# Partition sums on float32r halves, a softmax scale moved to ScalarE, and a later finish of one attention unit

## Chip, cores and metric

The kernel runs on one core of one Trainium2 chip. The metric is the device time of one execution in microseconds. The kernel before was run three times; its median is 651.46 us.

## What is computed

Two layers of an encoder on 512 tokens with 1024 features (cut from the reference):

```python
for l in range(DEPTH):                               # DEPTH = 2
    mod = silu(c) @ w_ada[l] + b_ada[l]              # 1024 -> 3072
    shift, scale, gate = split(mod, 3)
    h = rms_norm(x, norm_g[l]) * (1 + scale) + shift
    qa, ka, va, ga, qb, kb, vb, gb, qc, kc, vc, gc = split(h @ w_in[l])     # 3712 columns
    oa = rms_norm(diff_attention(qa, ka, va)) * silu(ga)  # A: 4 heads, p1 - lam * p2
    ob = dilated_attention(qb, kb, vb) * silu(gb)         # B: 6 heads, three window patterns
    oc = retention_bidir(qc, kc, vc) * silu(gc)           # C: 4 heads, chunked, two directions
    x = x + gate * (concat(oa, ob, oc) @ w_out[l])
```

All inputs are float32.

## The kernel before

**Products.** A dense product in float32 is made of three products on float32r: each operand is split into a high part, which ScalarE copies to float32r, and a low part, which VectorE subtracts (`split`, line 575; `Piece.split`, line 294, for weights). `products` (line 337) adds hi*hi, hi*lo and lo*hi in one accumulator of PSUM.

**Stages and groups.** The projection is cut by columns into chunks of 16 groups: 4 blocks of weight rows times 4 token tiles. A group is 6 products (2 row blocks of 128 times 3). In each layer the chunks are C's values and C's q and k (in layer 0 both in one chunk), A unit 0, B unit 0, A unit 1, B unit 1, B unit 2, gate C, then gate B (12 groups, turned), then the output projection (32 groups). A has 2 units of two heads, B has 3. Each chunk's accumulators come from a PSUM pool of 4 (`acc_p`). The scores have a PSUM pool of 2 (`sc_p`), the four-block transposes (`tr4`, line 569) a pool of 1 (`tr_p`), the values times weights one (`pv_p`).

**The plan.** `at(g, fn)` hangs a step behind group number g; `issue` (line 167) emits groups and their steps in that order, so it is a plan written out by hand with offsets such as `START_A1`, `GATE` or `FIN2`. The scheduler of the framework takes this order as a priority: on each engine it issues what is ready by its own model, and holds a step back until the buffers that it writes are free. So a step that stands later in the plan can be issued earlier, and a buffer that is held long moves what comes behind it. Each engine then works its own queue strictly in the issued order.

**Buffers that matter here.** The pool `ep` has five buffers of 128x512 with the tag "e" (line 144). The scores of A take four for a query tile (`Diff.scores`, line 738, tile e), those of B two (`Dilated.scores`, line 799, tile sb); they are free after the transposes of that tile. Also there: oat, oao and oasq (the finish of A's units, lines 755 to 764), cth (the gate of C, line 988) and several short-lived tiles. `out_pair(k)` (line 1018) gives the two float32r halves of a unit's output, in the single buffers s0 to s9, which C used earlier in the layer.

**A's finish.** `Diff.finish` (line 755) copies the output of the attention to oat; `finish2` (line 760), `FIN2` = 4 groups later, transposes it to oao, squares it on GpSimd and forms the norm; `finish3` (line 776), 12 groups later, applies the norm on VectorE and the gate values ga on GpSimd (line 781); `finish4` (line 783), 4 more later, transposes back and splits into the output pair. Both units have the same offsets.

**B's softmax.** For each query tile and head `Dilated.scores` makes the scores on TensorE (lines 802 and 803), adds the mask and takes the maximum in one VectorE instruction (line 807) and lets ScalarE take the exponential. `soft` (line 811) takes the reciprocal of the sum and scales the tile: head 0 on ScalarE, head 1 on VectorE (line 818), as `N_SOFT` is above any query tile. `turn` (line 699) transposes each head's tile, `values` (line 710) multiplies by v.

**Gate C and gate B.** `gate_done` (line 987) reads gate C's accumulator of a token tile: a tanh on ScalarE (cth), then two VectorE instructions. Gate B's products (lines 342 to 344) come next and need free accumulators.

**Sums over partitions.** `ada_steps` (line 455) forms a row of silu(c) @ w_ada: VectorE adds eight scaled weight rows per partition into `ada_acc` (line 474), and `end` (line 477) sums over the partitions and spreads the sum to all of them by one float32 product with a matrix of ones (line 479). It is used for the gate, twice in each layer (`gate_use`, line 1081, whose tile shares the two buffers "ga" with A's gate values), and for the modulation of layer 1, four times (`mod_use`, line 490). `plan_ada` (line 1087) sets its places. The sum stands in a score buffer of PSUM until it is read.

Of the kernel before, what the change touches and what calls it, by code (L numbers as in the profile page):

```python
# [9 lines left out]
F32 = mybir.dt.float32  # L10
# [7 lines left out]
S = 512  # L18
# [26 lines left out]
GATE, GATE_GAP, GATE_END = 55, 24, 18  # L45
GB_OUT = 9
SETUP, TABLES, RET_T, TAB1 = 12, 12, 19, 9      
N_A1, N_B1, N_SOFT = 5, 5, 9
E_T1, E_T2, E_X, E_QF, E_SCALE_A, E_SCALE_B = 1, 1, 1, 0, 0, 0
FIN2, FIN3, FIN4 = 4, 12, 16  # L50
X_BACK = 2


# [81 lines left out]
def encoder(ctx, tc, x, c, norm_g, w_ada, b_ada, w_in, w_out, params, consts, out):  # L135
# [19 lines left out]
    def act(o, i, f=AF.Copy, **kw):  # L155
        A.activation(o, i, f, **kw)  # L156
# [7 lines left out]
    def at(g, fn, *args):  # L164
        plan.setdefault(g, []).append((fn, args))
# [20 lines left out]
    cst = one.tile([P, N_KEEP], F32, name="cst")  # L186
    ones = one.tile([P, P], F32, name="ones")
    V.memset(ones, 1.0)
    nhalf = one.tile([P, 16], F32, name="nhalf")
    V.memset(nhalf, -0.5)  # L190

# [92 lines left out]
    class Piece:  # L284


        def __init__(self, src, n, where=None, gains=(None, None)):
            self.src, self.n, self.where, self.gains = src, n, where, gains
# [166 lines left out]
    def ada_steps(l, cols, use):  # L455

        (c0, n), cnt = cols[0], len(cols)
        step = cols[1][0] - c0 if cnt > 1 else 0
        z = {}

        def load(r):
            def fn():
                raw = z[r] = rp.tile([P, 2, 512], F32, name="raw")
                rows2(raw, w_ada, l * D * 3 * D + r * 3 * D + c0, KD * 3 * D, 3 * D, step, cnt, n)
                if r == 0:
                    a = z["a"] = two.tile([P, 512], F32, name="ada_acc")
                    G.memset(a, 0.0)
                    dma(a[0:1].rearrange("o (j n) -> o j n", j=cnt), dram(b_ada, l * 3 * D + c0, [[0, 1], [step, cnt], [1, n]]))
            return fn

        def add(r):
            def fn():
                for rr in range(2):
                    stt(z["a"], z[r][:, rr], cs[:, r + rr:r + rr + 1], z["a"], OP.mult, OP.add)
            return fn

        def end():
            ps = sc_p.tile([P, 512], F32, name="ada_ps", tag="sc")
            T.matmul(ps, ones, z["a"], start=True, stop=True)
            use(ps)  # L480
        return [load(r) for r in range(0, KD, 2)], [add(r) for r in range(0, KD, 2)], end

    mods = [None] * 4

# [234 lines left out]
                                 start=k == 0, stop=k == NT - 1)  # L719

    class Diff(Attention):
        def __init__(self, unit, g0, gap, oh, ol):
            self.oh, self.ol = oh, ol
            self.m = {}
            super().__init__(unit, g0, gap)

# [26 lines left out]
                self.e[qt, h] = self.m[2 * h]  # L753

        def finish(self, g):
            self.ob = ep.tile([P, S], F32, name="oat", tag="e")
            act(self.ob, self.pv)
            at(g + FIN2, self.finish2, g + FIN2)

        def finish2(self, g):  # L760
            ps = tr4([self.ob[:, tok_(t)] for t in range(NT)])
            o = self.o = ep.tile([P, 8, DV_A], F32, name="oao", tag="e")
            act(o.rearrange("p g d -> p (g d)"), ps.rearrange("p t m -> p (t m)"))
            sq = ep.tile([P, 8, DV_A], F32, name="oasq", tag="e")
            G.tensor_tensor(sq, o, o, OP.mult)
            ss = self.ss = sm.tile([P, 8], F32, name="oass")
            r0 = self.r0 = sm.tile([P, 8], F32, name="oar0")
            V.reciprocal(r0.rearrange("p (t h) -> p t h", h=2), self.ssum[:, :, 0::2])
            V.tensor_reduce(ss, sq, AX.X, OP.add)
            V.tensor_tensor(ss, ss, r0, OP.mult)  # L770
            V.tensor_tensor(ss, ss, r0, OP.mult)
            rms_end(ss, 8, DV_A)
            at(g + FIN3, self.finish3)
            at(g + FIN4, self.finish4)

        def finish3(self):
            o, ss = self.o, self.ss
# [5 lines left out]
        def finish4(self):  # L783
            on = self.o.rearrange("p (t h) d -> p t (h d)", h=2)
            ps = tr4([on[:, t] for t in range(NT)])
            split(self.oh, self.ol, ps.rearrange("p t m -> p (t m)"))

    class Dilated(Attention):
        def __init__(self, unit, g0, gap, ob, sg, out):
# [21 lines left out]
        def soft(self, qt):  # L811
            for h in range(2):
                V.reciprocal(self.s[h], self.s[h])
                sb = self.e[qt, h]
                if h == 0 or qt >= N_SOFT:
                    act(sb, sb, AF.Copy, scale=self.s[h])
                else:
                    V.tensor_scalar(sb, sb, self.s[h], None, OP.mult)

        def finish(self, g):  # L820
            if self.sg:
# [180 lines left out]
    def layer(l):  # L1002
# [15 lines left out]
        def out_pair(k):  # L1018
            oAB[k] = [one.tile([P, S], F32R, name=f"o{k}{z}", tag=f"s{2 * k + z}") for z in range(2)]
            return oAB[k]  # L1020

        def start_a(u, un, g, gap):
            Diff(un, g, gap, *out_pair(u))

        def start_b(u, un, g, gap):

# [58 lines left out]
            return use  # L1085

        def plan_ada(steps, g, gap, g_end=0):
            loads, adds, end = steps
            for i in range(4):
                at(g + gap * i - 6, loads[i])  # L1090
                at(g + gap * i, adds[i])
            at(max(g + gap * 4, g_end), end)
            return g + gap * 4

# [221 lines left out]
```

## Time and profile before

| | |
|---|---|
| three runs | 649.25, 651.46, 651.51 us (median 651.46) |
| the profiled execution | 650.6 us, span 648.7 us |
| mean granted TensorE clock | 0.992 |

The profile shows one execution. Busy shares of the engines are averages over all stages; a table by stretch gives them for one stage. A timeline lists instructions with start and duration in us, and in brackets the idle time of the engine before them with what ended it. Matmuls overlap in the records: the distance of their starts says what one costs in a dense stretch, its duration is longer. The chain of work that ended last gives these distances.

### The profile page before, as it was taken

The numbers are of one execution on the slowest core, as the hardware profiler recorded it, in microseconds if no ns is written. First come the engines' busy times: TensorE is split into PE (matmuls) and PEld (weight loads), VectorE is DVE, ScalarE is ACT, GpSimd is POOL, SyncE is SP. The second block draws the span as 40 slices with busy tenths as digits, with TensorE's granted clock in tenths as the row PEclk, the third lists the DMA queues.
The fourth block names the chain that finished last, engine by engine and source line by source line (L and its number), as shares of the span: only waits on it lengthen the run. The fifth ranks groups of instructions, "written<-read, shape, count | busy, mean of one in ns | idle before, by whom it ended". The sixth has DMA issues, their size and how long they took to land.

```text
span 648.7 us, 10469 instructions
## 1 busy us (share of the span) xinstructions
PE 622.2 (96%) x3487; PEld 512.2 (79%) x3487; DVE 491.8 (76%) x1206; ACT 344.4 (53%) x756; POOL 163.7 (25%) x183
## 2 busy tenths in 40 slices
PE   6899999999999996999999999999999999899997
PEld 1788888987888873677779998997788787677786
DVE  4787676689988987898969364768997997578443
ACT  4855263566646665564424344455756577566410
POOL 1105452514350510200411041633323340020000
PEclk9799999999999999999999999999999999999999
DMA  8998123535555556476643322235565453604211
GB/s 302 295 293 238 55 70 98 135 98 146 150 152 176 141 176 161 160 248 201 216 156 110 90 73 66 71 104 159 134 176 137 135 145 112 161 34 149 80 65 66
DMA packets 87277, 93.03 MB, mean 143 GB/s; under 512 B 7188, under 2 KB 68276, under 8 KB 87224
## 3 DMA queue, kind: packets, MB, share of 16 engines
q1 hardware_dynamic: 87224, 92.37, 48.0%
q8 instruction: 28, 0.46, 0.3%
q14 instruction: 25, 0.20, 0.1%
HBM read 72.42 MB, written 4.19 MB: 118 GB/s over the span
## 4 chain that ended last, share of the span: by engine, by line
PE 79%; DVE 9%; issue 4%; DMA 3%; POOL 3%; ACT 2%; SPq 1%; POOLq 0%; ACTq 0%
PE acc L346 16%; PE acc L348 16%; PE acc L347 16%; PE tr L572 8%; PE pv L718 5%; PE sc L741 2%; DMA x<-in_x_dram 2%; PE acc L344 1%; PE acc L342 1%; PE acc L343 1%; PE sc L802 1%; PE sc L803 1%; DVE wlo L315 1%; PE co L971 1%; DVE pt L708 1%
## 5 line engine op out<-in xcount | busy, mean ns | idle before, releaser
L346 PE MATMUL acc<-whi,hT 128*128 128x384 f32 (+1 forms) x424 | 154.7, 365 | 0.0
L347 PE MATMUL acc<-wlo,hT 128*128 128x384 f32 (+1 forms) x424 | 151.8, 358 | 0.0
L348 PE MATMUL acc<-whi,hL 128*128 128x384 f32 (+1 forms) x424 | 151.8, 358 | 0.0
L315 DVE TENSOR_TENSOR wlo<-raw,whi 128x384 fp32r<-128x384 f32 (+1 forms) x130 | 80.7, 650 | 26.7 <-ACT whi L156 26.4
L199 POOL TENSOR_TENSOR qkss<-qkss,nhalf 128x4 f32<-128x4 f32 (+1 forms) x40 | 52.6, 1315 | 128.3 <-DVE qkss L587 127.3
L346 PEld LDWEIGHTS acc<-whi,hT 128*128 128x128 f32 x424 | 80.0, 189 | 6.1
L348 PEld LDWEIGHTS acc<-whi,hL 128*128 128x128 f32 x424 | 79.8, 188 | 6.2
L347 PEld LDWEIGHTS acc<-wlo,hT 128*128 128x128 f32 x424 | 80.0, 189 | 5.5
L156 ACT ACTIVATE whi<-raw 128x768 fp32r<-128x768 f32 (+2 forms) x67 | 59.5, 890 | 39.7 <-PE acc L348 33.8
L159 DVE SCALAR_TENSOR_TENSOR ada_acc<-raw,cs,ada_acc 128x512 f32<-128x512 f32 x86 | 64.3, 749 | 3.9 <-DMA raw<-in_w_ada_dram 3.3
L156 ACT ACTIVATE e<-sc,mx 128x512 f32<-128x512 f32 x64 | 43.9, 689 | 35.5 <-DVE mx L743 16.9
L743 DVE TENSOR_REDUCE mx<-sc 128x1 f32<-128x512 f32 x64 | 43.5, 685 | 9.5 <-PE sc L741 8.8
L156 ACT ACTIVATE sb<-sb,mx 128x512 f32<-128x512 f32 x48 | 34.4, 717 | 20.4 <-DVE mx L807 20.2
L718 PE MATMUL pv<-pt,v 128*64 128x256 f32 x320 | 38.9, 385 | 1.0 <-DVE pt L708 0.9
L156 ACT ACTIVATE pt<-tr 128x512 f32<-128x512 f32 x40 | 23.8, 596 | 23.1 <-PE tr L572 22.9
L572 PE MATMUL tr<-cst,sb 128*128 128x128 f32 x192 | 30.7, 283 | 5.3 <-DVE nat L159 2.2
L807 DVE CUSTOM_DVE_ANT_0 sb<-sc,cst 128x512 f32<-128x512 f32 x48 | 32.1, 683 | 4.4 <-PE sc L803 2.6
L572 PEld LDWEIGHTS tr<-cst,sb 128*128 128x128 f32 x192 | 21.9, 142 | 16.0 <-ACT pt L156 7.7
L718 PEld LDWEIGHTS pv<-pt,v 128*64 128x64 f32 x320 | 21.2, 136 | 16.2 <-DVE pt L708 5.5
L708 DVE COPY pt<-tr 128x512 f32<-128x512 f32 x40 | 27.4, 684 | 7.8 <-PE tr L572 7.8
L639 POOL TENSOR_TENSOR qkn<-qkraw,qkss 128x256 f32<-128x256 f32 x40 | 30.0, 751 | 5.9 <-DVE qkraw L635 2.0
L741 PE MATMUL sc<-stk,stq 96*128 96x512 f32 x64 | 27.3, 434 | 1.0 <-ACT e L156 0.9
(294 smaller groups left out, 1367.8 us busy)
## 6 DMA issues: line engine op xcount, KB each, us to landing
raw<-in_w_ada_dram SPq DMA_DIRECT2D x64, 256.0 KB, 3.2
raw<-in_w_in_dram SPq DMA_DIRECT2D x48, 192.0 KB, 2.9
raw<-in_w_in_dram SPq DMA_DIRECT2D x24, 384.0 KB, 3.4
raw<-in_w_in_dram SPq DMA_DIRECT2D x32, 256.0 KB, 3.4
raw<-in_w_ada_dram SPq DMA_DIRECT2D x16, 512.0 KB, 5.1
raw<-in_w_out_dram SPq DMA_DIRECT2D x32, 256.0 KB, 3.0
x<-in_x_dram SPq DMA_DIRECT2D x8, 512.0 KB, 4.2
stB<-nat SPq DMA_DIRECT2D x32, 128.0 KB, 2.4
```

Source lines behind the costliest of these rows:

```text
L156: A.activation(o, i, f, **kw)
L159: V.scalar_tensor_tensor(o, a, s, b, op0, op1)
L199: G.tensor_tensor(o, i, nhalf[:, :n], OP.pow)
L315: V.tensor_tensor(l2[:, z], r2[:, z], h2[:, z].bitcast(F32), OP.subtract)
L346: T.matmul(ps, ah, hi[i], start=s_, stop=False)
L347: T.matmul(ps, ah, lo[i], start=False, stop=False)
L348: T.matmul(ps, al, hi[i], start=False, stop=e_)
L572: T.transpose(ps[:, i, :], b, ident)
L708: V.tensor_copy(pt, ps)
L718: T.matmul(self.pv[h * 64:h * 64 + 64, i * 256:i * 256 + 256], self.u.v[:, k, h * 64:h * 64 + 64], self.pt[h][:, k], start=k == 0, stop=k ...
L741: T.matmul(ps, self.u.stq[0:96, m, tok_(qt)], self.u.stk[0:96, m], start=True, stop=True)
L743: V.tensor_reduce(mx, ps, AX.X, OP.max, negate=True)
```

## The change

The sum over partitions is made of two float32r products: a new step `parts`, one group ahead, splits `ada_acc` into a high and a low half (two tiles of the pool `ep`), and `end` multiplies both with ones in float32r. `soft` scales both of B's heads on ScalarE. In A the tiles oat and oao go from the pool `ep` to the single buffers s1 and s0 (unit 0), s3 and s2 (unit 1), which the unit's output pair takes over in the last step, where the pair is now made. The offsets of the finish depend on the unit: those of unit 0 are as before, for unit 1 `finish2` comes 14 groups behind `finish` (4 before), `finish3` 6 behind that (12 before), `finish4` 9 (16 before).

```diff
-FIN2, FIN3, FIN4 = 4, 12, 16
+FIN_A = (4, 12, 16), (14, 6, 9)
...
+    ones_r = one.tile([P, P], F32R, name="ones_r")
+    V.tensor_copy(ones_r, ones)
...
         def end():
             ps = sc_p.tile([P, 512], F32, name="ada_ps", tag="sc")
-            T.matmul(ps, ones, z["a"], start=True, stop=True)
+            for i in range(2):
+                T.matmul(ps, ones_r, z["hl"][i], start=i == 0, stop=i == 1)
             use(ps)
-        return [load(r) for r in range(0, KD, 2)], [add(r) for r in range(0, KD, 2)], end
+
+        def parts():
+            z["hl"] = [ep.tile([P, 512], F32R, name="ada_hl", tag="e") for _ in range(2)]
+            split(*z["hl"], z["a"])
+        return [load(r) for r in range(0, KD, 2)], [add(r) for r in range(0, KD, 2)], parts, end
...
         def finish(self, g):
-            self.ob = ep.tile([P, S], F32, name="oat", tag="e")
+
+            self.ob = one.tile([P, S], F32, name="oat", tag=f"s{2 * self.k + 1}")
             act(self.ob, self.pv)
-            at(g + FIN2, self.finish2, g + FIN2)
+            at(g + self.fin[0], self.finish2, g + self.fin[0])
...
-            o = self.o = ep.tile([P, 8, DV_A], F32, name="oao", tag="e")
+            o = self.o = one.tile([P, 8, DV_A], F32, name="oao", tag=f"s{2 * self.k}")
...
-            at(g + FIN3, self.finish3)
-            at(g + FIN4, self.finish4)
+            at(g + self.fin[1], self.finish3)
+            at(g + self.fin[2], self.finish4)
...
-            split(self.oh, self.ol, ps.rearrange("p t m -> p (t m)"))
+            split(*self.out_pair(self.k), ps.rearrange("p t m -> p (t m)"))
...
                 sb = self.e[qt, h]
-                if h == 0 or qt >= N_SOFT:
-                    act(sb, sb, AF.Copy, scale=self.s[h])
-                else:
-                    V.tensor_scalar(sb, sb, self.s[h], None, OP.mult)
+                act(sb, sb, AF.Copy, scale=self.s[h])
...
+            at(max(g + gap * 4, g_end) - 1, parts)
             at(max(g + gap * 4, g_end), end)
```

## Rows read from the trace of the kernel before

**Rows 1.** The page: span, and busy us of each engine.
```profile
span 648.7 us, 10469 instructions
...
PE 622.2 (96%) x3487; PEld 512.2 (79%) x3487; DVE 491.8 (76%) x1206; ACT 344.4 (53%) x756; POOL 163.7 (25%) x183
```

**Rows 2.** Busy time by stretch: length, then PE, PEld, DVE, ACT, POOL; clock, DMA.
```profile
150.00:200.00 50.00, 48.30 (x297) 41.19 (x296) 45.39 (x125) 29.03 (x70) 23.55 (x27) 1.00 0.60 163
200.00:240.00 40.00, 38.91 (x235) 31.04 (x234) 36.04 (x90) 28.21 (x68) 11.50 (x18) 1.00 0.54 148
240.00:262.00 22.00, 16.30 (x91) 11.54 (x91) 17.48 (x42) 11.71 (x26) 1.04 (x1) 0.93 0.71 186
262.00:300.00 38.00, 37.37 (x193) 28.17 (x192) 35.86 (x77) 23.17 (x46) 4.26 (x4) 1.00 0.55 184
...
510.00:545.00 35.00, 34.86 (x207) 28.04 (x207) 32.00 (x82) 25.21 (x63) 7.38 (x8) 1.00 0.48 129
545.00:572.00 27.00, 24.27 (x152) 17.89 (x152) 17.34 (x47) 15.04 (x32) 2.74 (x2) 1.00 0.43 117
```

**Rows 3.** The same table, three shorter stretches.
```profile
244.40:259.50 15.10, 9.44 (x57) 5.54 (x56) 11.14 (x27) 8.30 (x18) 0.91 (x1) 0.98 0.69 170
258.90:262.30 3.40, 3.27 (x12) 2.18 (x10) 2.94 (x8) 1.38 (x3) 0.73 (x1) 0.50 0.90 259
...
559.00:567.60 8.60, 6.09 (x40) 3.69 (x40) 4.38 (x12) 4.79 (x11) 0.90 (x1) 1.00 0.80 198
```

**Rows 4.** Timeline of PE, layer 0: start, us, instruction, [idle before <- releaser].
```profile
244.22 0.33 PE L348 MATMUL acc<-whi,hL 128*128 128x384 f32 x1
...
257.22 0.66 PE L572 MATMUL tr<-cst,oat 128*128 128x128 f32 x4 [0.78 <-DVE pt L708]
...
259.54 0.79 PE L342 MATMUL acc<-hT,whi 128*128 128x512 f32 x1
```

**Rows 5.** Timeline of ACT, layer 0.
```profile
239.93 0.59 ACT L156 ACTIVATE oat<-pv 128x512 f32<-128x512 f32 x1
...
257.92 0.60 ACT L156 ACTIVATE oao<-tr 128x512 f32<-128x512 f32 x1 [2.19 <-PE tr L572]
258.41 0.49 ACT L156 ACTIVATE cth<-acc 128x384 f32<-128x384 f32 x1
```

**Rows 6.** Timeline of PE, layer 1.
```profile
558.56 0.34 PE L348 MATMUL acc<-whi,hL 128*128 128x384 f32 x1
...
567.64 0.50 PE L342 MATMUL acc<-hT,whi 128*128 128x512 f32 x1 [0.31 <-DVE cth L159]
```

**Rows 7.** Timeline of ACT, layer 1.
```profile
566.02 0.60 ACT L156 ACTIVATE oao<-tr 128x512 f32<-128x512 f32 x1 [2.19 <-PE tr L572]
566.52 0.49 ACT L156 ACTIVATE cth<-acc 128x384 f32<-128x384 f32 x1
```

**Rows 8.** The chain that ended last: start, us on the chain, what.
```profile
232.79 0.86 PE ada_ps L479 x2
...
273.33 0.23 PE acc L342
```

**Rows 9.** Groups by form: busy us, mean ns, idle before and releaser.
```profile
L818 DVE TENSOR_SCALAR sb<-sb,bs 128x512 f32<-128x512 f32 x24 | 11.6, 482 | 0.3
...
L577 DVE TENSOR_TENSOR o<-ob,o 128x512 fp32r<-128x512 f32 x4 | 2.7, 686 | 0.0
...
L156 ACT ACTIVATE sb<-sb,bs 128x512 f32<-128x512 f32 x24 | 17.2, 717 | 2.8 <-DVE bs L813 2.8
...
L156 ACT ACTIVATE whi<-raw 128x512 fp32r<-128x512 f32 x4 | 2.5, 618 | 0.0
```

**Rows 10.** Timeline of all engines, layer 0: the second gate value.
```profile
270.17 1.28 POOL L781 TENSOR_TENSOR oao<-oao,ga 128x512 f32<-128x512 f32 x1
...
271.49 0.60 ACT L156 ACTIVATE gate<-ada_ps 128x512 f32<-128x512 f32 x1 [1.50 <-POOL oao L781]
...
272.14 0.50 PE L802 MATMUL sc<-stk,stq 128*128 128x512 f32 x1 [0.63 <-ACT gate L156]
```

More of the change, by code (lines that the diff above doesn't have):

```diff
@@ L47 @@
 SETUP, TABLES, RET_T, TAB1 = 12, 12, 19, 9
-N_A1, N_B1, N_SOFT = 5, 5, 9
+N_A1, N_B1 = 5, 5
 E_T1, E_T2, E_X, E_QF, E_SCALE_A, E_SCALE_B = 1, 1, 1, 0, 0, 0
-FIN2, FIN3, FIN4 = 4, 12, 16
+FIN_A = (4, 12, 16), (14, 6, 9)
 X_BACK = 2
@@ L721, in encoder, with __init__ @@
     class Diff(Attention):
-        def __init__(self, unit, g0, gap, oh, ol):
-            self.oh, self.ol = oh, ol
+        def __init__(self, unit, g0, gap, fin, k, out_pair):
+            self.k, self.out_pair, self.fin = k, out_pair, fin
             self.m = {}
@@ L1022, in start_a @@
         def start_a(u, un, g, gap):
-            Diff(un, g, gap, *out_pair(u))
+            Diff(un, g, gap, FIN_A[u], u, out_pair)
         def start_b(u, un, g, gap):
@@ L1087, in plan_ada @@
         def plan_ada(steps, g, gap, g_end=0):
-            loads, adds, end = steps
+            loads, adds, parts, end = steps
             for i in range(4):
```

## The prediction

> **What bounds the kernel now.** I read the page's busy times first. TensorE is busy 622.2 us of a span of 648.7, VectorE 491.8, ScalarE 344.4 [rows 1]. So time can go in two ways only: TensorE gets less to do, or one of its gaps closes. The table by stretch then says where the gaps lie and what stands beside them [rows 2]. In most of layer 0 TensorE has little air (1.1 us idle of 40 between 200 and 240). Between 240 and 262 it is idle 22.00 - 16.30 = 5.7 us, and in layer 1 between 545 and 572 it is idle 2.7 us. Both stretches are the passage from B's second unit to the gate of C. VectorE is nearly full right behind the first of them: 35.86 of 38 us from 262 to 300. In layer 1 it has room.
>
> Two closer cuts show the holes themselves [rows 3]. From 244.4 to 259.5 TensorE works 9.44 of 15.10 us. From 258.9 to 262.3 its granted clock is 0.50, the lower level of 1.2 GHz, after that thin stretch; from 262.4 on it is not in these rows, and the whole stretch up to 300 reads 1.00 [rows 2]. From 559.0 to 567.6 it works 6.09 of 8.60 us, at full clock.
>
> What is it waiting for? The timeline of TensorE has its last projection product at 244.22 and the next one, on gate B, at 259.54 [rows 4]. Gate B needs accumulators, of which there are four, and these hold gate C until ScalarE has read them. ScalarE reads the first (cth) at 258.41, right behind oao [rows 5]. Before cth can be written it needs one of the five buffers "e" of the pool ep. B's second unit fills four with two query tiles, and A's second unit has the fifth: oat is written at 239.93 and read by its transposes at 257.22 [rows 4, 5]. So A's finish is in the way twice: by its buffer, and by its turn in ScalarE's queue. In layer 1 the same: last product 558.56, oao 566.02, cth 566.52, first product on gate B 567.64 [rows 6, 7].
>
> **The sums over partitions (part 1).** Eight sums are made, two for the gate in each layer and four for the modulation of layer 1. Each is a float32 product of 128x512 that takes two instructions and 0.86 us of the chain; a product of the same 512 columns on float32r operands takes 0.23 us [rows 8]. Two of these in place of one: 0.86 - 0.46 = 0.40 us, times 8 = 3.2 us. TensorE is full where most of them stand, so I take all of it: -3.2 us. The price is a split ahead of each: a ScalarE copy to float32r (0.618 us on 128x512) and a VectorE subtraction (0.686 us) [rows 9], 4.9 and 5.5 us in all, and 1.30 us more from the last addition to the product. They are hidden by the plan, which puts the split one group ahead of the product. If the cover is gone, as at the end of layer 0, where the next layer's h waits for the last modulation, up to 1.3 us come back once; I take none. The accumulator is released to the next memset on GpSimd by the split and no longer by the product. No DMA is added. The copy of the ones is one small VectorE instruction in a start that waits for loads.
>
> **B's second scale (part 2).** 24 multiplications leave VectorE, 0.482 us each, 11.6 us; 24 come to ScalarE, 0.717 us each, 17.2 us [rows 9]. With the splits, VectorE has 11.6 - 5.5 = 6.1 us less and ScalarE 17.2 + 4.9 = 22.1 us more, 366 in all. TensorE sees only when the second head's tile is ready for its transposes. The ScalarE scale can start earlier where VectorE's queue is full, and ends 0.24 us later where it isn't: between a gain of 24 x 0.482 = 11.6 (each on the path, which TensorE's gaps outside rows 3 don't allow) and a loss of 24 x 0.235 = 5.6. I take 0, as ScalarE has air beside it (28.21 of 40 and 25.21 of 35 us where B's and A's softmax run together [rows 2]).
>
> **A's second unit (part 3).** For unit 1 the transposes of the output move 10 groups back, the norm and gate product 4, the last transposes 3. Every instruction stays; none issues a DMA, so SP's queue is not touched. On GpSimd they pass the memset of the next modulation sum. oat and oao of both units leave the pool "e" for buffers of their own, so gate C has a buffer as soon as B's last query tile has its four, and cth has no oao ahead of it. Gate B's products then fill the gaps between B's transposes.
> - Layer 0: at least one round of transposes and eviction leaves the hole, 0.66 + 0.60 = 1.3 us [rows 4, 5]. At most the whole idle time goes, 5.7 us, and half of the 3.27 busy us at the low clock, 1.6: 7.3. I take -4.0, since the buffers come free only about halfway through the hole and VectorE is busy 11.14 of these 15.10 us [rows 3].
> - Layer 1: between 1.3 and 8.60 - 6.09 = 2.5 us; VectorE is half idle (4.38 us), so near the upper end: -2.0.
> - Elsewhere the freed buffers may help A's scores, which take four "e" a query tile. TensorE idles 1.7 us in 150 to 200 and 1.1 in 200 to 240 [rows 2]. Between 0 and 2.8: -1.0.
> - The new place: the second gate value needs the buffer of A's gate, which is free only after oao's product on GpSimd. Today its sum stands in one of two score buffers of PSUM from 232.79 to 271.49, and a score product waits 0.63 us for it [rows 8, 10]. Four groups later it stands there longer, and the rounds of oat and oao share the one transpose buffer with B's third unit. Between 0 and, with a wait like this at two query tiles in each layer and the two rounds of 1.3 us not hidden once, 4 x 0.63 + 2.6 = 5.1. TensorE has dense products there, so I take +1.0.
>
> **Sum.** -3.2 + 0 - 4.0 - 2.0 - 1.0 + 1.0 = -9.2 us. The profiled execution took 650.6 us (its span and 1.9 us around it), so 641.4; the median of the three runs, 651.46, lies 0.9 above, so 642.3 us.
>
> **Rivals.**
> (a) VectorE takes the gain of layer 0 back. For: from 240 to 300 it is busy 17.48 + 35.86 = 53.3 of 60 us, so a stretch shortened by more than its air runs into it. Against: some four to eight scales leave just there. Then layer 0 gives only its 1.3: -3.2 - 1.3 - 2.0 + 1.0 = -5.5, 646.0.
> (b) The freed buffer goes to the next score tile of B, not to cth, and gate B starts as late as before. For: gate C stands behind those tiles in the plan. Against: B has no further tile of unit 1 to place. -3.2 - 2 x 1.3 + 1.0 = -4.8, 646.7.
> (c) The score buffer held by the gate sum decides: 5.1 us instead of 1.0 and none of the gain elsewhere, with (a): -3.2 - 1.3 - 2.0 + 5.1 = -1.4, 650.1, no change.
> (d) Slower: ScalarE becomes the late one in B. The place is the softmax of a query tile: two exponentials, then both scales on one engine, with A's exponentials between them. If the second scale is waited for in full, each costs 0.717 us; from 9.2 / 0.717 = 13 of the 24 on, the whole gain is gone, and with 18 of them it is +12.9 - 9.2: 655.2. Against: ScalarE would be at about 57% of the span. The Trainium skill, ScalarE: Activation LUTs, section Rules for kernel authors, speaks for it: multiplications belong on VectorE, not on ScalarE. The trace agrees as to the durations (0.482 against 0.717 us); by that rule part 2 costs its 5.6 us and the sum is -3.6. That the change doesn't do what it says is not among the rivals, since the projections already run on float32r.
>
> **How the numbers follow.** A measurement of this kernel tells 0.5%, 3.3 us, from no change, so faster is below 648.2. Forecast 0.52; (a) 0.20; (b) 0.13; (c) 0.10; (d) 0.05. The forecast and (a) are faster but for their upper tails (0.01 and 0.03), (b) in three cases of four: 0.51 + 0.17 + 0.10 = 0.78. Same: these tails, 0.03 of (b) and (c): 0.16; slower: (d) and a little of (c), 0.06. The forecast's own range is 636 to 646: the lower end takes both holes in full (-3.2 - 7.3 - 2.5 - 2.8 + 1.0 = -14.8, 636.7). With (a), (b) and most of (c) it reaches 650: 636 to 650.
>
> **What would show it.** Right: the sums' products at 0.46 us a pair; in layer 0 the first cth and the first product on gate B some 7 to 10 us after the last gate C product, not 15; no second interval at half clock near 260; under 3 us of TensorE idle in the stretch that held 5.7; in layer 1 cth right behind B's transposes; ScalarE 366 and VectorE 486 us busy. Wrong: cth still behind the last transposes of B's second unit (b); a full VectorE ahead of TensorE's waits from 245 to 290 (a); score products that wait for the gate value longer than 0.63 us (c); transposes that wait for ScalarE's scale (d).

## The result and the profile after

The kernel after took 645.62 us (median of 4 runs, 644.64 to 646.41), the kernel before beside it 650.88 us (649.25 to 651.51): the ratio is 0.9922 (95% interval 0.99 to 0.9943). That is 5.1 us less (0.0078 x 651), where 9.2 were forecast. The profiled execution took 644.64 us, with a span of 642.9; it is the fastest of the four, with a mean granted clock of 0.989, where the other three have 0.984 to 0.986. The stretches below are read from one execution of each kernel, the times from the median of its runs.

The page of the kernel after, span and busy us of each engine, answers to [rows 1]:

```profile
span 642.9 us, 10490 instructions
...
PE 617.4 (96%) x3487; PEld 511.4 (80%) x3487; DVE 486.4 (76%) x1191; ACT 361.8 (56%) x788; POOL 164.1 (26%) x183
```

TensorE does 4.8 us less, VectorE 5.4 less, ScalarE 17.4 more. So the work did move as the diff says. What counts is where the span got shorter. For that I read five starts in TensorE's timeline: the first score of A and the first product on gate B in layer 0, the last output product of layer 0, and the same two starts in layer 1. In the kernel after (L748 is A's score, L344 gate B, L350 the third product of a projection):

```profile
125.60 0.40 PE L748 MATMUL sc<-stk,stq 96*128 96x512 f32 x1
...
255.33 0.40 PE L344 MATMUL acc<-hT,whi 128*128 128x512 f32 x1
...
338.30 0.39 PE L350 MATMUL acc<-wsp,o 128*128 128x512 f32 x1
...
429.68 0.39 PE L748 MATMUL sc<-stk,stq 96*128 96x512 f32 x1
...
560.02 0.40 PE L344 MATMUL acc<-hT,whi 128*128 128x512 f32 x1
```

Their distances cut the span into stretches, called a to e from here on: **a**, A's first score to gate B in layer 0; **b**, from there to the last output product; **c**, to A's first score in layer 1; **d**, to gate B there; **e**, to the end. Stretch c is 91.4 us in every kernel below.

| us | start | a | b | d | e | span |
|---|---|---|---|---|---|---|
| before | 126.6 | 133.0 | 82.7 | 134.1 | 81.1 | 648.7 |
| after | 125.6 | 129.7 | 83.0 | 130.3 | 82.8 | 642.9 |
| difference | -1.0 | -3.2 | +0.3 | -3.7 | +1.8 | -5.9 |

Both stretches that end at gate B are shorter, by 3.2 and 3.7 us, and behind gate B 2.1 us come back. Part of this is work that crossed the mark: gate B now starts ahead of some of B's transposes and ahead of A's round with oat. TensorE's groups by form in stretch e, before (one line) and after (two):

```profile
L572 PE MATMUL tr<-cst,sb 128*128 128x128 f32 x36 | 5.5, 275 | 0.1
```

```profile
L579 PE MATMUL tr<-cst,sb 128*128 128x128 f32 x44 | 6.6, 272 | 0.0
...
L579 PE MATMUL tr<-cst,oat 128*128 128x128 f32 x4 | 0.6, 272 | 0.0
```

Two rounds of four transposes of B and one of A have moved behind the mark; in layer 0 the counts are the same. At 0.44 us a round in a dense stretch (a line of the chain further down) that is 1.3 us in each layer, which is no gain. So a and b together are worth 2.9 us, d and e together 2.0. The start differs by up to 2.3 us between the profiles of this study, with nothing changed in it but one small copy, so I don't count it.

**Layer 0.** The windows of the kernel after, with the columns of [rows 2]:

```profile
240.00:262.00 22.00, 18.26 (x100) 11.96 (x98) 19.09 (x49) 15.82 (x35) 0.09 (x1) 0.84 0.74 202
...
545.00:572.00 27.00, 24.60 (x148) 18.64 (x147) 18.55 (x48) 20.14 (x42) 0.00 (x0) 1.00 0.40 105
...
247.40:254.20 6.80, 5.31 (x25) 2.86 (x23) 6.31 (x15) 4.49 (x10) 0.00 (x0) 0.50 0.79 175
```

TensorE's idle time in the first stretch fell from 5.7 to 3.7 us, but the mean granted clock fell as well, from 0.93 to 0.84 [rows 2]. In the second, in layer 1, it fell from 2.7 to 2.4 us only. From 247.4 to 254.2 the granted clock is 0.50, the lower level of 1.2 GHz, for 6.8 us; before, that interval was 3.4 us long [rows 3]. The timeline of TensorE in that hole shows what it did before and during it (L579 transposes, L725 values, L810 and L811 scores of B):

```profile
242.16 0.34 PE L350 MATMUL acc<-whi,hL 128*128 128x384 f32 x1
242.80 0.63 PE L579 MATMUL tr<-cst,qkn 128*128 128x128 f32 x4 [0.31 <-DVE pt L715]
...
244.84 0.50 PE L810 MATMUL sc<-stB,stC 128*128 128x512 f32 x1 [0.79 <-DVE mx L815]
...
246.72 0.50 PE L810 MATMUL sc<-stB,stC 128*128 128x512 f32 x1 [1.15 <-DVE mx L815]
...
248.93 1.11 PE L579 MATMUL tr<-cst,sb 128*128 128x128 f32 x4 [0.70 <-ACT pt L156]
250.83 3.61 PE L725 MATMUL pv<-pt,v 128*64 128x256 f32 x16 [0.78 <-DVE pt L715]
...
260.25 1.95 PE L725 MATMUL pv<-pt,v 128*64 128x256 f32 x16
```

The last gate C product stands at 242.16 and the first product on gate B at 255.33, 13.2 us later (15.3 before [rows 4]). The waits come ahead of the lower clock and at its beginning: scores wait for the VectorE instruction (mask and maximum) that frees their buffer, transposes and values for copies of pt. Of the 3.73 us of waits in these rows 3.03 are put down to VectorE, which is busy 6.31 of 6.80 us in the third window. The same sixteen products take 3.61 us at the lower level and 1.95 at the higher: in these products alone 1.7 us of the hole is the clock. Gate C is no longer what the hole waits for: VectorE's second reading of gate C's first accumulator, which frees it, is over at 251.77.

```profile
251.22 0.55 DVE L159 SCALAR_TENSOR_TENSOR cth<-cth,acc 128x384 f32<-128x384 f32 x1
```

The product on gate B stands in TensorE's queue behind the sixteen products, a round of transposes and two scores, and by the trace waits for nothing but them.

ScalarE in the same hole shows that the order did change as meant:

```profile
250.34 0.46 ACT L156 ACTIVATE cth<-acc 128x384 f32<-128x384 f32 x1
250.88 0.72 ACT L156 ACTIVATE sb<-sb,bs 128x512 f32<-128x512 f32 x1
252.93 0.49 ACT L156 ACTIVATE cth<-acc 128x384 f32<-128x384 f32 x1 [1.33 <-DVE cno L997]
```

The first cth comes 8.2 us behind the last gate C product, where it was 14.2 [rows 4, 5], and no oao stands ahead of it. In layer 1 it comes 3.2 us behind (556.34 after 553.16), where it was 8.0 [rows 6, 7].

### The profile page after: what moved, and what is told of

Its sections match the earlier page's. It is cut to its first block, busy times and chain, and to the rows that moved or that the text cites. A ratio compares the mean times of both kernels' runs of the same rounds, so it can differ in the third digit from the quotient of the medians.

```text
span 642.9 us, 10490 instructions
## 1 busy us (share of the span) xinstructions
PE 617.4 (96%) x3487; PEld 511.4 (80%) x3487; DVE 486.4 (76%) x1191; ACT 361.8 (56%) x788; POOL 164.1 (26%) x183
## 4 chain that ended last, share of the span: by engine, by line
PE 78%; DVE 9%; DMA 4%; issue 3%; ACT 2%; POOL 1%; SPq 1%; DVEq 0%; ACTq 0%; POOLq 0%
PE acc L348 16%; PE acc L350 16%; PE acc L349 15%; PE tr L579 8%; PE pv L725 5%; PE sc L748 2%; DMA raw<-in_w_ada_dram 2%; DMA raw<-in_w_in_dram 2%; DVE ada_acc L159 1%; PE acc L346 1%; PE acc L344 1%; PE acc L345 1%; DVE wlo L317 1%; PE sc L810 1%; PE co L976 1%
## 5 line engine op out<-in xcount | busy, mean ns | idle before, releaser
L350 PE MATMUL acc<-whi,hL 128*128 128x384 f32 (+1 forms) x424 | 152.0, 358 | 0.0
L201 POOL TENSOR_TENSOR qkss<-qkss,nhalf 128x4 f32<-128x4 f32 (+1 forms) x40 | 53.1, 1328 | 125.6 <-DVE qkss L594 100.4
L350 PEld LDWEIGHTS acc<-whi,hL 128*128 128x128 f32 x424 | 79.9, 188 | 6.3
L725 PE MATMUL pv<-pt,v 128*64 128x256 f32 x320 | 40.6, 398 | 2.7 <-DVE pt L715 2.5
L725 PEld LDWEIGHTS pv<-pt,v 128*64 128x64 f32 x320 | 21.8, 141 | 18.3 <-DVE pt L715 7.9
L156 ACT ACTIVATE sb<-sb,bs 128x512 f32<-128x512 f32 x48 | 33.2, 713 | 2.2 <-DVE bs L821 1.9
L579 PE MATMUL tr<-cst,sb 128*128 128x128 f32 x192 | 30.3, 282 | 2.5 <-ACT pt L156 1.4
L579 PEld LDWEIGHTS tr<-cst,sb 128*128 128x128 f32 x192 | 22.2, 143 | 11.5 <-ACT pt L156 5.4
```

The costliest lines, as they stand in the source:

```text
L201: G.tensor_tensor(o, i, nhalf[:, :n], OP.pow)
L350: T.matmul(ps, al, hi[i], start=False, stop=e_)
L579: T.transpose(ps[:, i, :], b, ident)
L725: T.matmul(self.pv[h * 64:h * 64 + 64, i * 256:i * 256 + 256], self.u.v[:, k, h * 64:h * 64 + 64], self.pt[h][:, k], start=k == 0, stop=k ...
```

## The experiments

Part 1 is the sums, part 2 B's second scale on ScalarE, part 3 A's finish with its new offsets and buffers. All ratios are to the kernel before on the same chip, with the 95% interval; "us" behind a ratio is its distance from 1 times 651.

### Each part alone

Each kernel is the kernel before with one part of the diff.

```diff
...
+            for i in range(2):
+                T.matmul(ps, ones_r, z["hl"][i], start=i == 0, stop=i == 1)
...
```

> The kernel before with part 1 alone (sums over partitions from two float32r halves). Theory H (the sums give what the products save, the holes are part 3's): eight times 0.40 us less on TensorE, -2.5 to -3.2 us against the kernel before; the pair of products at 0.46 us; the holes before gate B unchanged. Rival S (the scale on ScalarE is what costs): the same, -3. Rival O (what moves the time is how the issue order falls out anew, not the terms): no relation to 3.2, anywhere from -4 to +2.

Part 1 alone: 653.44 us, ratio 1.0024 (1.0008 to 1.0041), +1.6 us. Theories H and S, which wanted about -3, miss; only the wide range of O holds.

```diff
-                if h == 0 or qt >= N_SOFT:
-                    act(sb, sb, AF.Copy, scale=self.s[h])
-                else:
-                    V.tensor_scalar(sb, sb, self.s[h], None, OP.mult)
+                act(sb, sb, AF.Copy, scale=self.s[h])
```

> The kernel before with part 2 alone (both of B's heads scaled on ScalarE). H: no change, within 1 us, VectorE 480 and ScalarE 362 us busy. S: slower by 1 to 3 us, with transposes of B waiting for ScalarE's scale. O: anywhere from -2 to +2.

Part 2 alone: 654.97 us, 1.0053 (1.0031 to 1.0075), +3.5 us: slower, and by a little more than S said.

```diff
-FIN2, FIN3, FIN4 = 4, 12, 16
+FIN_A = (4, 12, 16), (14, 6, 9)
...
-            self.ob = ep.tile([P, S], F32, name="oat", tag="e")
+            self.ob = one.tile([P, S], F32, name="oat", tag=f"s{2 * self.k + 1}")
```

> The kernel before with part 3 alone (A's finish in buffers of its own, unit 1's steps later). H: both holes before gate B shorter by some 2 us each, about 3 us given back behind them because the second gate value is written some 13 us later and holds its score buffer: -1.5 to -2.5 us. S: the giving back is the scale's, so without it -4 to -6 us. O: anywhere from -4 to +2.

Part 3 alone (oao likewise): 643.92 us, 0.988 (0.9861 to 0.9898), -7.8 us. It is worth more than the whole change, and more than any of the three theories allowed.

So two of the three parts cost time by themselves. Their spans show where:

| us | a | b | d | e |
|---|---|---|---|---|
| before | 133.0 | 82.7 | 134.1 | 81.1 |
| part 1 alone | 134.5 | 80.2 | 138.4 | 81.1 |
| part 2 alone | 134.3 | 81.0 | 139.2 | 82.6 |
| part 3 alone | 128.4 | 84.5 | 128.6 | 83.2 |

Parts 1 and 2 gain some 2 us in b and lose 4.4 and 5.1 us in d, the passage of layer 1. With part 1 alone, TensorE waits there like this:

```profile
559.91 0.75 PE L579 MATMUL tr<-cst,sb 128*128 128x128 f32 x4 [2.03 <-DVE nat L159]
561.34 1.11 PE L579 MATMUL tr<-cst,sb 128*128 128x128 f32 x4 [0.69 <-ACT pt L156]
568.30 0.66 PE L579 MATMUL tr<-cst,sb 128*128 128x128 f32 x4 [0.22 <-ACT pt L156]
569.74 0.66 PE L579 MATMUL tr<-cst,oat 128*128 128x128 f32 x4 [0.78 <-DVE pt L715]
571.08 0.66 PE L579 MATMUL tr<-cst,sb 128*128 128x128 f32 x4 [0.69 <-ACT oao L156]
572.05 0.50 PE L344 MATMUL acc<-hT,whi 128*128 128x512 f32 x1 [0.31 <-DVE cth L159]
```

This hole is the one of [rows 6], longer: A's round with oat still stands ahead of gate B, and the clock is at its lower level for 6.8 us of it, which it was not in layer 1 before.

The clock has a share in these two losses. The executions of one kernel differ in their mean granted clock, and the time goes with it: on this chip the kernel before took 649.28 us in an execution at 0.992 and 653.66 to 654.02 in three at 0.987. Part 1 alone stands at 0.986 in nine of its twelve executions (652.24 to 654.93 us; the kernel before at 0.986: 651.72 and 653.23), part 2 alone runs from 651.94 at 0.991 to 658.74 at 0.983. At the same clock little is left of the first loss, and about half of the second (estimated from these executions). Whether the longer holes bring the clock down or the clock makes them longer is not shown.

### Part 3 taken apart

The buffers alone, with both units' offsets as they were (against part 3 alone):

```diff
-FIN_A = (4, 12, 16), (14, 6, 9)
+FIN_A = (4, 12, 16), (4, 12, 16)
```

> The kernel before with the buffers of part 3 alone (oat and oao out of the pool of five; all steps of the finish where they were). H: cth can be written before oao, the holes get shorter by 1 to 2 us each, and the second gate value comes no later than before (271 and 574 us), so nothing is given back: -2 to -4 us, better than part 3 whole. If the offsets are what counts, no change, within 1 us, with cth still right behind oao.

649.94 us, 0.9966 (0.9951 to 0.9981), -2.2 us. The time lies in the range of theory H, but not for its reason: the first cth of layer 0 stays at 257.9, right behind oao. Where the 2.2 us are gained stays open, as the one profile is of the slowest execution (651.03 us) and shows no gain in its span. Here too the clock is lower than before, 0.983 to 0.987.

The offsets alone, with oat and oao still in the pool of five (the diff is against part 3 alone):

```diff
-            self.ob = one.tile([P, S], F32, name="oat", tag=f"s{2 * self.k + 1}")
+            self.ob = ep.tile([P, S], F32, name="oat", tag="e")
...
-            o = self.o = one.tile([P, 8, DV_A], F32, name="oao", tag=f"s{2 * self.k}")
+            o = self.o = ep.tile([P, 8, DV_A], F32, name="oao", tag="e")
```

> The kernel before with the later offsets of A's second unit alone; oat and oao stay in the pool of five. Theory B (it is the pool's fifth buffer that counts, and with oat in it for 10 groups longer gate C has none): the hole ahead of gate B in layer 0 stays at 15 us or grows, 651 to 656 us. Theory Q (it is the turn in ScalarE's queue that counts, the buffer follows by itself, as cth may now take what B's second unit frees): the first cth near 250 in layer 0 and near 556 in layer 1, 643 to 646 us, as with the whole of part 3 (643.9).

648.96 us, 0.9958 (0.9941 to 0.9974), -2.7 us: neither theory. TensorE and then ScalarE at the end of its hole in layer 0:

```profile
256.21 0.66 PE L572 MATMUL tr<-cst,sb 128*128 128x128 f32 x4
...
257.55 0.66 PE L572 MATMUL tr<-cst,sb 128*128 128x128 f32 x4 [0.22 <-ACT pt L156]
258.53 0.51 PE L342 MATMUL acc<-hT,whi 128*128 128x512 f32 x1 [0.32 <-DVE cth L159]
```

```profile
256.90 0.60 ACT L156 ACTIVATE pt<-tr 128x512 f32<-128x512 f32 x1 [1.97 <-PE tr L572]
257.39 0.49 ACT L156 ACTIVATE cth<-acc 128x384 f32<-128x384 f32 x1
```

The round with oat is gone from the hole (compare [rows 4]), and no oao stands ahead of cth. But cth still waits until the first head of B's last query tile has been transposed (256.21 to 256.87). With the same offsets and oat in a buffer of its own (the whole of part 3) it comes 7.9 us earlier:

```profile
249.50 0.47 ACT L156 ACTIVATE cth<-acc 128x384 f32<-128x384 f32 x1
```

So the buffer is what holds it here; that it is the fifth one, held by oat, I read from the plan. The two halves of part 3 do different things: the offsets take a round of some 1.3 us out of the way, and with them the buffers let cth pass B's last tile, which the buffers alone don't, as oao is then in the way. Alone they give 2.7 and 2.2 us, together 7.8.

### Two parts together, and the sums' halves in buffers of their own

The halves of the sums take two of the five buffers that B's softmax and cth live on. To see what that costs, the halves of the two gate sums of a layer go to s8 and s9, the modulation's stay in the pool:

```diff
-            z["hl"] = [ep.tile([P, 512], F32R, name="ada_hl", tag="e") for _ in range(2)]
+            z["hl"] = [one.tile([P, 512], F32R, name="ada_hl", tag=f"s{8 + i}") if own else
+                       ep.tile([P, 512], F32R, name="ada_hl", tag="e") for i in range(2)]
```

Parts 3 and 1:

> Parts 3 and 1 together (the change without part 2). Theory P (part 1 loses because its halves take two of the five buffers e just where B's and A's tiles need them): no better than part 3 alone, 644 to 646 us. Theory X (what the whole change lacks against part 3 alone is the scale on ScalarE): better than part 3 alone by 1 to 2.5 us, 641.5 to 643. Theory C (parts 1 and 2 alone were slow because a longer hole before gate B in layer 1 let TensorE's clock fall there): as X, as part 3 has closed that hole.

644.17 us, 0.9888 (0.9865 to 0.991), -7.3 us.

Parts 3 and 2:

> Parts 3 and 2 together (the change without part 1). P: the scale costs nothing, 643 to 644.5 us, as part 3 alone. X: slower than part 3 alone by 1.5 to 3.5 us, 645.5 to 647.5, and the first product on gate B in layer 1 comes later. C: as part 3 alone, within 1 us.

648.48 us, 0.9957 (0.9943 to 0.9971), -2.8 us.

Part 1 alone with buffers of its own:

> The kernel before with part 1 alone, but the halves of the four gate sums in the single buffers s8 and s9, idle there, and no longer in the pool of five (the modulation sums' halves stay in it). P: the loss of part 1 alone goes, -1.5 to -3 us against the kernel before, and gate B in layer 1 starts as before or earlier. X and C: it is not the pool but the split ahead of the product or the clock; +1 to +2 us as part 1 alone.

648.64 us, 0.9962 (0.9948 to 0.9976), -2.5 us.

Parts 3 and 1 with buffers of their own:

> Parts 3 and 1 with the halves of the gate sums in s8 and s9. P: the best so far, 2 to 3 us under part 3 alone, 641 to 642. X and C: the same as parts 3 and 1 with the halves in the pool, within 0.7 us.

642.81 us, 0.9876 (0.9859 to 0.9893), -8.1 us.

Three things follow. The two pool buffers that the gate's sums take cost part 1 4.1 us when it stands alone (+1.6 against -2.5, intervals apart). Beside part 3 they cost nothing that can be told (-7.3 against -8.1). And part 2 costs 5.0 us on top of part 3 (-7.8 against -2.8), with intervals far apart. That is not the clock: at 0.989 part 3 took 643.27 to 643.61 us, parts 3 and 2, on another chip, 648.98. No theory holds whole. P has the price of the pool right where part 1 stands alone and misses the price of part 2; X has that price in kind, though larger than it said, and wanted a gain of part 1 on part 3 that isn't there; C falls with the slow kernel of parts 3 and 2 and the fast one of part 1 in buffers of its own. The last kernel beats both the kernel before and the kernel after.

### Where part 2 costs

Part 3 with both scales on ScalarE only for B's second unit (the one of the passage), or only for the first and the third:

```diff
-                if h == 0 or qt >= N_SOFT:
+                if h == 0 or self.k == 1:
```

> Part 3, and both scales on ScalarE for B's second unit alone, 8 of the 24. Theory U (the price of part 2 is paid in the passage to gate C, whose length B's second unit sets): nearly all of the 4.6 us between 643.9 (part 3) and 648.5 (parts 3 and 2) is here, 647 to 648.5 us, and the first product on gate B some 2 us later than with part 3 alone in layer 1. Theory E (each scale costs its share, wherever it stands): a third of it, 645.4 us. Theory V (the price is paid where B stands beside A's softmax or the dense products, units 0 and 2): 643.9 us.

643.65 us, 0.9883 (0.9866 to 0.99), -7.6 us: the same as part 3 alone.

```diff
-                if h == 0 or qt >= N_SOFT:
+                if h == 0 or self.k != 1:
```

> Part 3, and both scales on ScalarE for B's first and third unit, 16 of the 24. Theory U (paid in the passage): 643.9 us, as part 3 alone. Theory E (each its share): 647.0 us. Theory V (paid beside A and the dense products): 648.5 us, and the first product on gate B in layer 1 against the last gate C product as with part 3 alone.

648.71 us, 0.9962 (0.9947 to 0.9976), -2.5 us: the whole price. Theory V is right as to the place and theory U is wrong: it is not the unit of the passage that pays. Which of the other two units pays is not told apart by a run. The groups by form show who waits, first with part 3 alone, then with the second unit's scales moved, then with the other two units' (busy us, mean ns, then idle time of TensorE ahead of B's transposes, by releaser):

```profile
L572 PE MATMUL tr<-cst,sb 128*128 128x128 f32 x192 | 30.3, 280 | 3.2 <-DVE nat L159 1.9 <-ACT pt L156 1.3
```

```profile
L572 PE MATMUL tr<-cst,sb 128*128 128x128 f32 x192 | 30.8, 283 | 3.1 <-DVE nat L159 1.8 <-ACT pt L156 1.2
```

```profile
L572 PE MATMUL tr<-cst,sb 128*128 128x128 f32 x192 | 30.7, 284 | 6.0 <-ACT pt L156 3.4 <-DVE nat L159 2.6
```

TensorE's idle time ahead of B's transposes nearly doubles, and most of what is new is waited for on ScalarE. The longest of these waits is in layer 1, in the third unit. ScalarE and TensorE of the last kernel there:

```profile
589.59 1.34 ACT L156 ACTIVATE sb<-sb,bs 128x512 f32<-128x512 f32 x2
591.94 0.60 ACT L156 ACTIVATE gate<-ada_ps 128x512 f32<-128x512 f32 x1 [1.01 <-POOL oao L781]
...
594.52 0.64 ACT L156 ACTIVATE whi<-raw 128x512 fp32r<-128x512 f32 x1
595.04 0.60 ACT L156 ACTIVATE pt<-tr 128x512 f32<-128x512 f32 x1
```

```profile
592.64 0.60 PE L572 MATMUL tr<-cst,sb 128*128 128x128 f32 x4
...
595.70 0.66 PE L572 MATMUL tr<-cst,sb 128*128 128x128 f32 x4 [1.52 <-ACT pt L156]
```

The first head's transposes start at 592.64 and last 0.60 us. Their eviction pt is ready to go then, but ScalarE comes to it only at 595.04, behind the gate value and five other instructions, and the second head's transposes wait 1.52 us for the one transpose buffer. With part 3 alone the gate value waits 0.34 us and the same pt starts at 591.36, 0.73 us behind the start of its transposes.

The scale itself (0.71 us) is not what TensorE waits for at this place: both scales are done at 590.93, and ScalarE then idles 1.01 us, because the gate value waits for GpSimd's product on oao.

```profile
590.18 1.73 POOL L781 TENSOR_TENSOR oao<-oao,ga 128x512 f32<-128x512 f32 x1 [2.15 <-DVE bs L814]
```

That product ends 29.6 us behind the start of gate B, with part 3 alone 27.6 (587.60 against 559.97). Its input is written by VectorE, whose small steps of the norm stand between other instructions here and together there. So I put this wait down to the order of the queues, which moving the scales changed, and not to the 0.71 us that each adds. Why TensorE pays some 5 us in all, and why the whole of part 2 doesn't show this one wait, but others in d, I can only put down to the new order; no run isolates it.

### The second gate sum later

The best kernel so far, with the second gate sum later, so that it holds no score buffer. The expectation speaks of 30 groups; by the plan it is 27, from 15 ahead of gate B to 12 behind its start:

```diff
-            plan_ada(ada_steps(l, [(2 * D + hf * 512, 512)], gate_use(hf), True), g_gb - GATE + GATE_GAP * hf, 4, g_gb - GATE_END + hf)
+            plan_ada(ada_steps(l, [(2 * D + hf * 512, 512)], gate_use(hf), True), g_gb - GATE + GATE_GAP * hf, 4, g_gb + (12 if hf else -GATE_END))
```

> Parts 3 and 1, the halves of the gate's sums in buffers of their own, and the second gate sum 30 groups later in the plan, behind oao's last use on GpSimd, so that it should hold no score buffer while it waits for the buffer of A's gate. Theory G (the held score buffer costs B's third unit some 1 us a layer, as the plan for the new place said): 641 us, 1.5 to 2 under the same kernel with the sum at its old place (642.8). Theory N (B's third unit has room there, TensorE has dense products to take): 642.8 us, no difference over 0.6 us.

644.83 us, 0.99 (0.9882 to 0.9919), -6.5 us: no gain, rather 2 us lost (the two intervals overlap). The stretch that the move was meant for, e, is 83.3 us as without it (83.2), though it now holds one sum more, which left d (126.7 against 128.3 us). The loss is elsewhere, in b (86.9 against 83.0 us), at a modulation sum near the end of layer 0:

```profile
329.91 0.79 PE L482 MATMUL ada_ps<-ada_hl,ones_r 128*128 128x512 f32 x1 [3.17 <-ACT ada_hl L156]
```

TensorE waits 3.17 us for the ScalarE copy of the high half, and ScalarE had first waited for weights (3.89 us) and for the residual that closes the layer. That is the price that part 1 can have when its cover is gone. Parts 3 and 1 with the halves in the pool pay it as well, in the same place:

```profile
326.15 0.79 PE L482 MATMUL ada_ps<-ada_hl,ones_r 128*128 128x512 f32 x1 [2.18 <-ACT ada_hl L156]
```

So the time of this run can't decide between theories G and N: without that wait it would lie about where G had it. What speaks against G's reason is the trace: in none of the kernels with part 3 whose waits I read does a product of TensorE wait for the score buffer that the gate sum holds (the lines with part 3 alone stand below).

## Why the prediction was right, and where its steps were not

The direction and the range held, the place of the gain too. The size was forecast at -9.2 us and is -5.1. That the time came out inside the range is in part luck: part 3 gave more than forecast, parts 1 and 2 less, and the range of 14 us has room for two of the rivals too. Rival (a)'s 646.0 us is nearer to the 645.62 measured than the forecast's 642.3, though not by its terms.

In runs, one part after the other: part 3 gives -7.8, part 1 in the pool on top of it +0.5 (not told from nothing), part 2 on top of both +2.2 (-7.3 to -5.1; these two intervals overlap a little). In the other order part 2 on part 3 is a clear +5.0, and part 1 on both -2.3 (-2.8 to -5.1; here the intervals just touch). So how the missing 4.1 us divide between parts 1 and 2 depends on the order. The +2.2 go with the clock, too: parts 3 and 1 have executions from 0.987 to 0.995, the kernel after 0.984 to 0.989, and at 0.989, where they meet, the first took 644.7 and 645.18 us, the second 644.64.

**What bounds the kernel: right.** The holes ahead of gate B were most of the time to be had. One reading is off: gate C's accumulators are freed by VectorE's reading behind cth (the first product on gate B waits for "DVE cth" [rows 6]), not by ScalarE's. Part 3 closes the one in layer 1 altogether: TensorE is busy 27.00 of 27 us with part 3 alone in the second of these windows (24.27 before [rows 2]).

```profile
240.00:262.00 22.00, 18.36 (x95) 12.86 (x95) 19.16 (x46) 11.46 (x25) 0.00 (x0) 0.84 0.83 230
...
545.00:572.00 27.00, 27.00 (x163) 20.86 (x161) 19.92 (x52) 17.46 (x36) 0.00 (x0) 1.00 0.43 117
```

**Part 1, "TensorE is full where most of them stand, so I take all of it": this step failed.** The saving per sum is as forecast. The chain of the kernel after has a pair at 0.46 us. It also has the price of the values, of a score product and of a round of transposes (0.44 us in a dense stretch, 0.59 behind the values):

```profile
262.68 0.46 PE ada_ps L482 x2
...
542.14 1.88 PE pv L725 x16
544.02 0.59 PE tr L579 x4
544.60 0.24 PE sc L810
...
548.31 0.44 PE tr L579 x4
```

But the gate's four sums stand ahead of the passages, and there the time is not TensorE's. With part 3, and the halves in buffers of their own, part 1 brings the last gate C product of layer 0 forward from 115.9 to 114.3 us behind A's first score, and yet the first product on gate B goes back from 128.4 to 129.4: the hole grows from 12.5 to 15.2 us. Stretch d gives 0.2 of the expected 0.8. The modulation's four sums are in stretch b, which goes from 84.5 to 83.0 us, about their 4 x 0.40. On top of part 3 the whole part gave 0.3 us by the ratios, in place of 3.2. In other company it gives more: 2.5 us on the kernel before with the halves in buffers of their own, again in b (80.0 against 82.7 us; a and d are longer), and 2.3 us on parts 3 and 2. So a price per sum, times eight, is not what the runs show. The second omission is the pool: the step priced the split of each sum, and not that its two halves take two of five "e" buffers. Alone that cost 4.1 us. The third is the split at the end of layer 0: "up to 1.3 us come back once" was too low a bound, as TensorE waits 2.2 us for it with parts 3 and 1 in the pool (b is 86.8 us there) and 3.2 in the last experiment; in the kernel after it is 0.4.

**Part 2, "I take 0": this step failed as well.** Its bounds held (-11.6 to +5.6): alone it costs 3.5 us, on part 3 it costs 5.0. I argued that ScalarE has air beside it. The air was there, but a share of busy time says nothing of the order in a queue. Rival (d) had the engine right for most of the new waits, and the price not: it put the wait on the scale itself, 0.717 us each. Measured are some 5 us for the 16 scales of the first and third unit, 0.3 us each, and nothing for the 8 of the second; at the wait that was looked at, the scale was not what ScalarE was late by. The Trainium skill, ScalarE: Activation LUTs, section Rules for kernel authors, puts multiplications on VectorE. By that rule part 2 costs its 5.6 us; the runs show a price for the first and the third unit, above their 16 x 0.235 = 3.8 us, and none for the second, in whose passage in layer 0 VectorE is the fuller engine (17.48 against 11.71 us of 22 [rows 2]).

**Part 3, -6.0 in sum: right in sum, not in its terms.** Measured -7.8, in the profile (the slowest of six executions) -6.0 from a to e. Three rounds of transposes, 1.3 us, cross from a to b and from d to e, as in the kernel after. By stretches of the profile with part 3 alone:
- Layer 0, hole and elsewhere, -4.0 and -1.0: stretch a is 4.6 us shorter, 1.3 of them the rounds that crossed. So 3.3 of the 5.0 us are there. That VectorE limits this hole is right.
- Layer 1, -2.0 with 2.5 as the upper end: d is 5.5 us shorter. The bound was wrong, as it took TensorE's busy time in a thin stretch for its work. From the end of the last gate C product to gate B there are 8.74 us [rows 6]. The work in it is five rounds of transposes, four score products and one of values: 5 x 0.44 + 4 x 0.24 + 1.88 = 5.0 us at the chain's distances. So the hole was worth 3.7, not 2.5, and the three rounds that crossed make another 1.3: 5.0.
- The new place, +1.0: b and e are 1.9 and 2.2 us longer, of which 2 x 1.3 is the three rounds. Of A's two rounds only the one with oat comes here; the one with oao stood behind gate B before, too (288.06 and 593.42 us). The rest, some 1.5 us, was to be +1.0. It isn't the held score buffer, for which no product waits here: TensorE's waits in the new place, with part 3 alone, are for VectorE's maximum and for copies of pt.

```profile
279.93 0.50 PE L802 MATMUL sc<-stk,stq 128*128 128x512 f32 x1 [0.76 <-DVE mx L807]
290.19 0.66 PE L572 MATMUL tr<-cst,sb 128*128 128x128 f32 x4 [0.58 <-ACT pt L156]
292.70 0.63 PE L572 MATMUL tr<-cst,oao 128*128 128x128 f32 x4 [0.46 <-DVE pt L708]
...
582.87 0.50 PE L802 MATMUL sc<-stk,stq 128*128 128x512 f32 x1 [0.52 <-DVE mx L807]
```

**The rivals.** (a) holds in part: the waits of layer 0's hole are mostly on VectorE. (b) fell: cth did get the buffer, and needs both halves of part 3 for it. (c) fell with the waits just shown: the 0.63 us for the gate value [rows 10] are gone, not longer. (d), a price of part 2, is part of what is missing; how much depends on the order in which the parts are taken.

**The signs given.** Right: the sums' pairs, the first cth of layer 0 8.2 us behind gate C, cth without oao ahead of it in layer 1, VectorE at 486 us, ScalarE near 366 (361.8). Wrong: gate B 7 to 10 us behind gate C in layer 0 (13.2, as it stands behind the values and not behind cth), no second interval at half clock (it is twice as long), under 3 us of idle time (3.7). The distance from gate C to gate B tests little: with parts 3 and 1 in buffers of their own this hole is 15.2 us and the kernel is the fastest, since whatever brings gate C forward also lengthens the hole. The distance from A's first score is the better measure, together with a count of what crossed the mark.

## What to carry to other kernels

An engine's air in a table of busy shares is no cover for a moved instruction: 16 moved scales cost some 5 us here on an engine that was busy for half of the span, the same move of the other 8 nothing. Look at what the move does to the order of the queues, and at waits for a third engine in them, and try the parts of a move apart. Time saved on the bound engine ahead of a hole is lost in the hole, unless the hole's end moves too; so first find what sets that end. When two kernels are compared by marks in a timeline, count the work that crossed a mark. And count the buffers of a new step like its instructions: two tiles in a pool of five cost more here than the products saved, where the step stood alone.

## What the chip showed that was not expected

- Busy time of TensorE in a thin stretch is more than its work: 6.09 us busy [rows 3] for some 5.0 us at dense distances.
- The granted clock stood at 0.50 for 6.8 us in the kernel after and with part 3 alone, although the idle time around it was less than before, where it was 3.4 us. The values' sixteen products cost 3.61 us at that level and 1.95 at the other. Closing a hole in part did not keep the clock up; in layer 1, where part 3 alone closed it entirely, the clock stayed at 1.00, but so it did in the kernel after, with 2.4 us of idle time there, and before. What decides this stays open.
- Two halves of one part gave 2.7 and 2.2 us alone and 7.8 together: a wait with two causes shows most of its price only when both are gone. The lower clock of the buffers alone (0.983 to 0.987, with the whole part 0.988 to 0.989) has a share in that.
